# Attention: the transposes of a pair of query tiles, and their products with V, each begun only when the operands of all of them are there

## The chip, the cores and the metric

One core of a Trainium2 chip runs the whole program. The metric is device time in microseconds of one execution, compared as medians. Before the change the median of 3 runs is 2395.19 us (2393.38 to 2398.52).

## The reference, cut to what matters

The program is one step of a two-layer encoder over 2048 prompt frames and 32 sample frames, width 1024. Layer 0 is sliding-window attention, layer 1 a gated DeltaNet. The change touches layer 0 alone. There 16 query heads share 4 key and value heads of width 64. A chunk of 64 frames reads itself and the 128 frames before it:

```python
s = jnp.einsum('bnqkgd,bnskd->bnkgqs', q, k) * (HEAD_DIM ** -0.5)
s = s - slopes * dist                      # ALiBi, then -inf outside the window
m = jnp.maximum(jnp.max(s, axis=-1, keepdims=True), sink)
p = jnp.exp(s - m)
den = jnp.sum(p, axis=-1, keepdims=True) + jnp.exp(sink - m)
o = jnp.einsum('bnkgqs,bnskd->bnqkgd', p / den, v)
y = (o * jax.nn.silu(gate)) @ w_out
```

All is fp32. The big projections (`h @ w_in`, `@ w_out`) are each split into three products of rounded parts.

## The kernel before, in words

**Tiling.** The tokens are cut into 4 slabs of 512 (the second carries the 32 sample frames too). Each slab's attention runs over 20 projection blocks of 128 output columns: for each of two groups of heads a key block, a value block, and four times a query block and a gate block. A block is 24 matmuls of up to 512 columns into bank `pj` (`project`, line 624), so TensorE has a stream of projection work. Output blocks (`out_blocks`, line 865) of an earlier slab are mixed in. Then comes the DeltaNet stage, which does not run the changed function.

**A pair of query tiles.** After each gate block `attention` (line 1188) spawns side jobs: for a prompt slab two calls of `attend` (line 1064), each for two query tiles of 128 frames and the two heads of one index `i`; in the second slab one more, for the 32 sample frames. That makes 64 calls for pairs of tiles and 8 for the sample frames. At most three calls are under way at a time. In one call, in this order:

1. scores into two `ta` banks, bias and row maximum into `s` on VectorE (DVE), one of four units (two tiles times two heads) at a time;
2. exponentials of the four units on ScalarE (ACT), sums into `den`;
3. four `tensor_scalar` on DVE, `s<-s,den`, one for each unit: the scaling by 1/den;
4. for each tile: take a `tb` bank, four transposes of 128x128 (`tb<-con,s`; two key blocks times two heads), one ACT copy of the bank to SBUF (`pt<-tb`), give the bank back, and let the projection go on before the next tile (`yield 0`);
5. for each tile: four products with V (`tc<-pt,vt`, stationary V of 64 columns, so output goes to one half of the partitions), then again `yield 0` before the next tile. Each fp32 product stands as two matmul records, so one tile is 8 records and a pair is 16;
6. `of<-tc,sg` on DVE, rounding on ACT, remainder on GpSimd (POOL), and the call counts as attended.

**What sets the order.** Nothing is issued when the Python code runs. Each call of an engine becomes an `Op` (line 196) in `Order` (line 211), with a rank by the order of emission. A side job is advanced between two projection matmuls (`step`, line 465), by a clock that `Estimate` (line 77) keeps with costs per operation; a bare `yield` there waits until the job's last operation is estimated done, and `yield 0` waits for nothing but lets the projection emit its next matmul first. At the end of a stage `flush` (line 299) plays the engines forward in estimated time: an operation becomes ready when those it depends on have ended plus a lag, and of the ready ones of an engine the lowest rank goes first. That fixes each engine's program order. On the chip each instruction waits for its own semaphores only, in that order.

**Costs in the plan.** `Estimate.COST` (line 88) gives a DVE scaling of 256 columns with a per-partition scalar 68 + 0.52 x 256 + 60 = 261 ns, and an ACT copy of 512 columns from PSUM 52 + 0.83 x 512 = 477 ns; `cost` (line 119) gives a projection matmul of 512 columns 216 ns and knows no price for going from one form of matmul to another.

**Banks.** `BANKS` (line 441) gives `ta` and `tb` two banks each and `tc` one. `bank` (line 516) takes one bank when one is free; `both` (line 523) waits until none is held and takes two. Before the change only the scores use `both`.

Of the kernel before, what the change touches and what calls it, by code (L numbers as in the profile page):

```python
# [3 lines left out]

# [1 line left out]

# [10 lines left out]
P = 128  # L17
# [5 lines left out]
CH = 64  # L23
# [33 lines left out]
class Block:  # L57
# [3 lines left out]
    def __init__(self, src, run, need=None, ahead=None, pre=None, post=None, ks=range(KT)):  # L61
        self.beside = False
        self.src, self.run, self.need, self.ahead, self.pre, self.post, self.ks = src, run, need, ahead, pre, post, ks
# [132 lines left out]
class Op:  # L196


    def __init__(self, engine, call=None, cost=0.0, dma=False):
        self.engine, self.call, self.cost, self.dma = engine, call, cost, dma  # L200
        self.after, self.left, self.ends, self.done, self.rank = [], 0, {}, False, 0


class Place:
# [6 lines left out]
class Order:  # L211
# [9 lines left out]
    def __init__(self, est):  # L221
        self.est = est
        self.ops, self.log, self.places, self.rings = [], {}, {}, {}
        self.free, self.dma, self.rank = dict.fromkeys(self.ENGINES, 0.0), 0.0, 0
        self.lead, self.past = 0, []

    def place(self, pool, tag, bufs, name):
        ring = self.rings.setdefault((id(pool), tag), [])
# [21 lines left out]
    def add(self, op, ins, outs):  # L250
        self.rank += 1
        op.rank = (self.rank - self.lead, self.rank)
        self.ops.append(op)
        waits = {}
        for x, w in [(x, False) for x in ins] + [(x, True) for x in outs]:
            name = x.tensor.name
            if name in self.places:
                self.places[name].ops.append(op)
            elif not name.startswith(SCRATCH):
                continue  # L260
            a = self.region(x)
            bank = x.space == bass.MemoryType.PSUM
            log = []
            for b, bw, o in self.log.get(name, []):
                meet = a[0] < b[1] and b[0] < a[1] and (bank or a[2] < b[3] and b[2] < a[3])
                if o is not op and ((w or bw) and meet or bank and o.engine != op.engine):
                    waits[id(o)] = o
                    if w and a[0] <= b[0] and b[1] <= a[1] and a[2] <= b[2] and b[3] <= a[3]:
                        continue
                log.append((b, bw, o))  # L270
            self.log[name] = log + [(a, w, op)]
        for o in waits.values():
            self.link(o, op)
        if op.engine == "tensor":
            self.past.append((self.est.at("tensor"), op))
        elif op.dma:
            i = bisect.bisect(self.past, min(self.est.at("tensor") - self.EARLY, self.START), key=lambda x: x[0])
            if i:
                self.link(self.past[i - 1][1], op)
# [19 lines left out]
    def flush(self):  # L299

        overs = []
        for p in self.places.values():
            if p.old and p.over is None:
                p.over = Op(None)
                overs.append(p.over)
                for o in p.old.ops:
                    self.link(o, p.over)
                for o in {id(o): o for o in p.ops}.values():
                    self.link(p.over, o)
        self.wait = {e: [] for e in self.ENGINES}  # L310
        ready = {e: [] for e in self.ENGINES}
        for o in [o for o in overs + self.ops if o.left == 0]:
            self.settle(o)
        while any(self.wait.values()) or any(ready.values()):
            when = {e: max(self.free[e], 0.0 if ready[e] else self.wait[e][0][0]) for e in self.ENGINES if ready[e] or self.wait[e]}
            e = min(when, key=when.get)
            now = when[e]
            while self.wait[e] and self.wait[e][0][0] <= now:
                _, rank, o = heapq.heappop(self.wait[e])
                heapq.heappush(ready[e], (rank, o))  # L320
            _, op = heapq.heappop(ready[e])
            op.call()
            if op.dma:
                self.free[e] = now + 60
                self.dma = max(now + 1500, self.dma) + op.cost * (self.CLOSE if now < self.START else 1)
                op.ends = {"dma": self.dma + 500}
            else:
                self.free[e] = now + op.cost
                op.ends = {e: self.free[e]}
            op.start = now  # L330
            self.finish(op)
        assert all(o.done for o in self.ops)
        self.ops = []
# [49 lines left out]
class Kern:  # L383
# [680 lines left out]
    def attend(self, me, i, q, sg, gp, vt, og, m, pairs, keyn, tiles, ocol):  # L1064
# [10 lines left out]
        s = self.t(ap, [P, 4, WIN], "s", bufs=3)[:m]  # L1075
# [3 lines left out]
        banks = yield from self.both("ta")  # L1079
        for a, (qc, kc, lo) in enumerate(pairs):  # L1080
            for n, (part, k) in enumerate(((0, kh), (0, kl), (1, kh))):
                for x, ps in enumerate(banks):
                    rows = slice(x * CH, (x + 1) * CH)
# [26 lines left out]
            nc.vector.tensor_scalar(out=s[:, u, lo:keyn], in0=s[:, u, lo:keyn], scalar1=unit(den, u), scalar2=None, op0=ALU.mult)  # L1110
        yield
        pts = []
        for a, tl in enumerate(tiles):
            ps = yield from self.bank("tb")
            pt = self.t(ap, [P, 2, 2, P], "pt", bufs=4)
            for jj, (blk, vidx, rows) in enumerate(tl):
                for x in range(2):
                    at = (jj * 2 + x) * P
                    self.tp(ps[:rows, at : at + m], s[:, 2 * a + x, blk * P : blk * P + rows])
            if len(tl) == 2 and m == P:  # L1120
                ev = [(pt.rearrange("p a b t -> p (a b t)"), ps)]
            else:
                ev = [(pt[:r, j, :, :m], ps[:r, j * 2 * P : (j + 1) * 2 * P].rearrange("p (x t) -> p x t", x=2)[:, :, :m])
                      for j, (_, _, r) in enumerate(tl)]
            for dst, src in ev:
                nc.scalar.copy(dst, src)
            pts.append((a, pt, tl))
            self.give("tb")
            yield 0
        yield  # L1130
        yield from og.wait()
        po = yield from self.bank("tc")
        for a, pt, tl in pts:
            for x in range(2):
                for jj, (blk, vidx, rows) in enumerate(tl):
                    self.mm(
                        po[x * CH : (x + 1) * CH, a * P : a * P + m], vt[:rows, vidx, x * CH : (x + 1) * CH],
                        pt[:rows, jj, x, :m], jj == 0, jj == len(tl) - 1)
            yield 0
        yield  # L1140
        n = (np_ - 1) * P + m
        of = self.t(ap, [P, 2 * P], "of", bufs=2)
# [806 lines left out]
    def last_outs(self, si, slab, og, over):  # L1949
# [7 lines left out]
        def sink(f, two, y, cols):  # L1957

            ys[f] = two, y
            acc = accs[halves.index(cols)]  # L1960
            add = (lambda st, x, i, first=False, last=False:
                   self.mm(st[:, 0:1], x[:, i * P : (i + 1) * P], self.ones[:, 0:1], first, last))
            if f == 0:
                acc.n, acc.sts, acc.scaled = 0, [], () if acc is accs[0] else (1, 4, 6)
                if acc is accs[0]:
                    for x in ("acc", "rb", "xa"):
                        yield from self.take(x)
                acc.t = self.t(self.xp, [P, 544], "acc" if acc is accs[0] else "rb", bufs=1)[:, : n // 2]
                if acc is accs[1]:
                    for bank in ("ms", "tc"):  # L1970
                        acc.sts.append((yield from self.bank(bank)))
            yield y
            sq = self.t(self.xp, [P, 544], "xa", bufs=3)[:, : n // 2] if f else acc.t
            self.nc.scalar.activation(sq, y[:, cols], AF.Square)
            yield
            if f and not (acc.sts and f >= POOLED):
                (nc.gpsimd if acc.sts else nc.vector).tensor_tensor(out=acc.t, in0=acc.t, in1=sq, op=ALU.add)
            elif f:
                for i, st in enumerate(acc.sts):
                    if f == KT - 1:  # L1980
                        add(st, acc.t, i)
                    add(st, sq, i, f == POOLED, f == KT - 1)
            if f in acc.scaled:
                self.nc.scalar.activation(y[:, cols], y[:, cols], AF.Copy, scale=self.par[:, PC_FG + f : PC_FG + f + 1])
            acc.last = acc.sts[1] if acc.sts else acc.t
            acc.n += 1
# [248 lines left out]
```

## Time and profile before

| | |
|---|---|
| median of 3 runs | 2395.19 us |
| the profiled execution, its own time | 2401.5 us |
| its span, first to last instruction | 2399.7 us |
| mean granted TensorE clock | 0.971 of 2.4 GHz |
| attention stage | about the first 940 us |
| products with V, records (attention only) | 1056, from 50.4 to 932.2 us |
| instructions of the span | 44456 |

The span is 1.8 us shorter than the execution's own time. PE is TensorE's matmuls, PEld its weight loads. In a timeline of PE a row is a run of like matmuls; the start of the next row less the start of this one is what the run took of TensorE's time, since the printed duration holds the pipeline's tail as well. A mark in square brackets at the end of a row is idle time ahead of it and the engine that ended it.

### The profile page before, as it was taken

What the parts mean: (1) busy time and instruction counts of PE and PEld (TensorE: products, weight loads), DVE (VectorE), ACT (ScalarE), POOL (GpSimd) and SP (SyncE); (2) the same over time, 40 slices, a digit from 0 to 9 for tenths busy, and PEclk for the clock granted to TensorE, in tenths of its full rate; (3) what the DMA queues carried; (4) which work ended last, traced back from release to release, by engine and by line L of the source; (5) the groups of instructions that cost most, each with busy time, mean ns of one, the idle gap of its engine ahead of it and who ended that gap; (6) DMA issues with size and microseconds to landing.
All of it is one profiled execution on the core that took longest, in us unless ns stands there. A gap on an engine that the chain in (4) does not pass through costs nothing.

```text
span 2399.7 us, 44456 instructions
## 1 busy us (share of the span) xinstructions
PE 2279.1 (95%) x14759; PEld 1851.9 (77%) x14759; DVE 1644.0 (69%) x5024; ACT 1265.6 (53%) x3792; POOL 864.4 (36%) x1044
## 2 busy tenths in 40 slices
PE   8999999899999999999999999999999999999997
PEld 5667888797778777777779798876798777777776
DVE  6765465726562546488888768888786888886876
ACT  5555465636553555355666454674554466445533
POOL 4566555565554333223322122331312222222222
PEclk9998999999999999999999999998999989999998
DMA  7565755476525124644334564334456634466541
GB/s 253 167 190 181 240 181 177 150 252 213 176 89 164 63 64 135 199 159 139 121 109 133 181 226 154 120 99 136 138 162 213 213 113 139 138 212 214 159 141 67
DMA packets 222832, 382.75 MB, mean 159 GB/s; under 512 B 29922, under 2 KB 45194, under 8 KB 222602
## 3 DMA queue, kind: packets, MB, share of 16 engines
q1 hardware_dynamic: 220154, 377.75, 49.4%
q8 instruction: 116, 1.90, 0.3%
q10 hardware_dynamic: 2448, 2.16, 0.3%
q14 instruction: 114, 0.93, 0.1%
HBM read 311.63 MB, written 68.19 MB: 158 GB/s over the span
## 4 chain that ended last, share of the span: by engine, by line
PE 57%; DVE 24%; ACT 7%; issue 3%; DMA 3%; POOL 2%; SPq 0%; DVEq 0%; ACTq 0%; POOLq 0%
PE pj L185 41%; PE tb L185 6%; PE ta L185 5%; PE tc L185 4%; DVE cy L185 3%; DVE s L185 3%; DVE sub L185 2%; DVE tl L185 2%; ACT s L185 1%; DVE ml L185 1%; ACT ta L185 1%; DVE r L185 1%; DVE mx L185 1%; DVE md L185 1%; DVE xa L185 1%
## 5 line engine op out<-in xcount | busy, mean ns | idle before, releaser
L185 PE MATMUL pj<-hk,wh 128*128 128x512 f32 (+1 forms) x8184 | 1796.7, 365 | 23.1 <-DVE xr L185 6.8
L185 PEld LDWEIGHTS pj<-hk,wh 128*128 128x128 f32 x8184 | 1331.4, 192 | 237.2 <-issue 22.9
L185 POOL TENSOR_TENSOR wh<-wr,wh 128x512 fp32r<-128x512 f32 x224 | 295.3, 1321 | 333.2 <-ACT wh L185 282.0
L185 DVE SCALAR_TENSOR_TENSOR cy<-cx,cw,cy 128x512 f32<-128x512 f32 x360 | 230.8, 651 | 45.0 <-ACT cy L185 40.3
L185 ACT CAST wh<-wr 128x512 fp32r<-128x512 f32 x224 | 137.7, 617 | 215.3 <-PE pj L185 164.3
L185 ACT ACTIVATE s<-s,mx 128x256 f32<-128x256 f32 (+1 forms) x272 | 132.0, 487 | 32.3 <-DVE mx L185 32.0
L185 ACT ACTIVATE qs<-tb,egq 64x128 f32<-64x128 f32 x264 | 95.8, 363 | 88.4 <-DVE r L185 76.0
L185 DVE TENSOR_SCALAR s<-s,den 128x256 f32<-128x256 f32 (+1 forms) x272 | 133.6, 542 | 1.3
L185 DVE TENSOR_TENSOR sub<-ml,tl 128x60 f32<-128x60 f32 (+24 forms) x527 | 126.5, 240 | 10.2
L185 ACT ACTIVATE cx<-cy 128x512 f32<-128x512 f32 (+1 forms) x96 | 61.1, 636 | 130.9 <-DVE cy L185 104.4
L185 DVE TENSOR_TENSOR tl<-tl,sub 128x60 f32<-128x60 f32 (+24 forms) x527 | 122.8, 233 | 10.0
L185 POOL TENSOR_TENSOR pr<-pr,ph 128x512 fp32r<-128x512 f32 x82 | 111.2, 1356 | 40.6 <-ACT ph L185 37.7
L185 DVE CUSTOM_DVE_ANT_0 s<-ta,bias 128x256 f32<-128x256 f32 (+1 forms) x272 | 96.3, 405 | 39.3 <-PE ta L185 38.0
L185 POOL COPY cx<-hist 128x3 f32<-128x3 f32 x96 | 26.7, 278 | 264.3 <-DVE kq L185 62.7
L185 DVE TENSOR_TENSOR xr<-pj,xr 128x512 f32<-128x512 f32 (+1 forms) x72 | 41.2, 577 | 108.3 <-PE pj L185 72.1
L185 POOL TENSOR_TENSOR so<-so,mhalf 128x4 f32<-128x4 f32 x33 | 36.8, 1114 | 218.0 <-DVE so L185 190.2
L185 DVE SCALAR_TENSOR_TENSOR r<-tb,nbk,vb 64x128 f32<-64x128 f32 x264 | 91.8, 348 | 29.9 <-PE tb L185 25.3
L185 ACT ACTIVATE qs<-o 128x128 f32<-128x128 f32 x132 | 40.7, 308 | 133.4 <-DVE o L185 128.1
L185 ACT COPY cx<-pj 128x512 f32<-128x512 f32 (+2 forms) x149 | 64.1, 446 | 78.9 <-PE pj L185 63.5
L185 PE MATMUL tc<-pt,vt 128*64 128x128 f32 (+2 forms) x1056 | 91.3, 289 | 12.1 <-ACT pt L185 11.3
L185 PE MATMUL tb<-st,kq 128*128 128x128 f32 x512 | 95.7, 289 | 6.4 <-DVE st L185 5.7
L185 PEld LDWEIGHTS tb<-st,kq 128*128 128x128 f32 x512 | 83.4, 196 | 21.3 <-DVE st L185 13.1
(242 smaller groups left out, 3578.6 us busy)
## 6 DMA issues: line engine op xcount, KB each, us to landing
wh<-xswwd SPq DMA_DIRECT2D x528, 256.0 KB, 2.9
wr<-in_wa SPq DMA_DIRECT2D x160, 256.0 KB, 2.9
wh<-xswwdo SPq DMA_DIRECT2D x112, 256.0 KB, 2.9
pr<-in_wd SPq DMA_DIRECT2D x66, 256.0 KB, 4.0
xswwd<-ph SPq DMA_DIRECT2D x66, 256.0 KB, 2.7
xswwd<-pr SPq DMA_DIRECT2D x66, 256.0 KB, 3.6
wr<-in_wao SPq DMA_DIRECT2D x64, 256.0 KB, 2.9
xa<-in_x SPq DMA_DIRECT2D x48, 256.0 KB, 3.3
```

Of the source, the lines that this page charges most:

```text
L185: self.order.add(Op(self.name, lambda: call(*args, **kw), cost, op == "dma_start"), ins, outs)
```

## The change

`Order` gets groups. `together()` opens one: a group is an `Op` without an engine, and every TensorE operation that is added while it is open depends on it, while it depends on all that these wait for outside the group. So in the plan no operation of the group is ready before all of their operands are, and their banks free. The group is only in the plan: no instruction and no semaphore is added on the chip. In `attend`, the two `tb` banks are taken at once with `both`, the eight transposes of a pair form one group, then the two copies follow and both banks are given back; the products with V of the pair form a second group. The two `yield 0` go.

```diff
+    @contextmanager
+    def together(self):
+
+        self.gang = Op(None)
+        self.ops.append(self.gang)
+        yield
+        self.gang = None
...
+        if self.gang and op.engine == "tensor":
+            op.gang = self.gang
+            self.link(op.gang, op)
         for o in waits.values():
             self.link(o, op)
+            if op.gang and o.gang is not op.gang:
+                self.link(o, op.gang)
...
                 for o in {id(o): o for o in p.ops}.values():
                     self.link(p.over, o)
+                    if o.gang:
+                        self.link(p.over, o.gang)
...
         pts = []
-        for a, tl in enumerate(tiles):
-            ps = yield from self.bank("tb")
+        banks = yield from self.both("tb")
+        with self.issue.together():
+            for a, (ps, tl) in enumerate(zip(banks, tiles)):
+                for jj, (blk, vidx, rows) in enumerate(tl):
+                    for x in range(2):
+                        at = (jj * 2 + x) * P
+                        self.tp(ps[:rows, at : at + m], s[:, 2 * a + x, blk * P : blk * P + rows])
+        for a, (ps, tl) in enumerate(zip(banks, tiles)):
             pt = self.t(ap, [P, 2, 2, P], "pt", bufs=4)
-            for jj, (blk, vidx, rows) in enumerate(tl):
-                for x in range(2):
-                    at = (jj * 2 + x) * P
-                    self.tp(ps[:rows, at : at + m], s[:, 2 * a + x, blk * P : blk * P + rows])
...
             pts.append((a, pt, tl))
+        for _ in banks:
             self.give("tb")
-            yield 0
         yield
         yield from og.wait()
         po = yield from self.bank("tc")
-        for a, pt, tl in pts:
-            for x in range(2):
-                for jj, (blk, vidx, rows) in enumerate(tl):
-                    self.mm(
-                        po[x * CH : (x + 1) * CH, a * P : a * P + m], vt[:rows, vidx, x * CH : (x + 1) * CH],
-                        pt[:rows, jj, x, :m], jj == 0, jj == len(tl) - 1)
-            yield 0
+        with self.issue.together():
+            for a, pt, tl in pts:
+                for x in range(2):
+                    for jj, (blk, vidx, rows) in enumerate(tl):
+                        self.mm(
+                            po[x * CH : (x + 1) * CH, a * P : a * P + m], vt[:rows, vidx, x * CH : (x + 1) * CH],
+                            pt[:rows, jj, x, :m], jj == 0, jj == len(tl) - 1)
         yield
```

## Rows read from the trace of the kernel before

**Rows 1.** The page: busy time by engine, and the chain that ended last.
```profile
PE 2279.1 (95%) x14759; PEld 1851.9 (77%) x14759; DVE 1644.0 (69%) x5024; ACT 1265.6 (53%) x3792; POOL 864.4 (36%) x1044
...
PE 57%; DVE 24%; ACT 7%; issue 3%; DMA 3%; POOL 2%; SPq 0%; DVEq 0%; ACTq 0%; POOLq 0%
```

**Rows 2.** Busy by stretch: window, length, PE, PEld, DVE, ACT, POOL, PEclk, DMA, GB/s.
```profile
0.00:940.00 940.00, 891.13 (x5729) 711.91 (x5730) 517.87 (x1514) 509.16 (x1337) 487.66 (x420) 0.98 0.52 167
940.00:2400.00 1460.00, 1387.94 (x9032) 1140.02 (x9030) 1126.16 (x3511) 756.44 (x2455) 376.70 (x624) 0.97 0.49 154
460.00:475.00 15.00, 11.10 (x56) 7.64 (x54) 12.36 (x37) 8.60 (x29) 8.65 (x9) 0.77 0.46 141
711.00:717.00 6.00, 6.00 (x53) 4.64 (x52) 2.13 (x6) 3.15 (x8) 2.01 (x2) 1.00 0.23 72
780.00:935.00 155.00, 154.24 (x992) 116.74 (x991) 86.41 (x314) 87.05 (x247) 56.15 (x50) 1.00 0.21 67
```

**Rows 3.** PE timeline, products with V: the first and the last run of 116.
```profile
50.45 0.44 PE L185 MATMUL tc<-pt,vt 128*64 128x128 f32 x4 [1.30 <-ACT pt L185]
...
931.92 0.67 PE L185 MATMUL tc<-pt,vt 128*64 128x128 f32 x8
```

**Rows 4.** PE timeline of 782 to 796 us: two pairs of tiles, in part.
```profile
782.76 5.12 PE L185 MATMUL pj<-hk,wh 128*128 128x512 f32 x21
787.72 0.60 PE L185 MATMUL tb<-con,s 128*128 128x128 f32 x4
788.08 0.48 PE L185 MATMUL pj<-hk,wh 128*128 128x512 f32 x1
788.39 0.60 PE L185 MATMUL tb<-con,s 128*128 128x128 f32 x4
788.75 1.17 PE L185 MATMUL pj<-hk,wh 128*128 128x512 f32 x4
789.85 1.14 PE L185 MATMUL tc<-pt,vt 128*64 128x128 f32 x16
790.92 0.51 PE L185 MATMUL pj<-hk,wh 128*128 128x512 f32 x1
...
792.94 0.67 PE L185 MATMUL tc<-pt,vt 128*64 128x128 f32 x8
793.53 0.50 PE L185 MATMUL pj<-hk,wh 128*128 128x512 f32 x1
793.97 0.67 PE L185 MATMUL tc<-pt,vt 128*64 128x128 f32 x8
794.56 1.66 PE L185 MATMUL pj<-hk,wh 128*128 128x512 f32 x6
```

**Rows 5.** PE timeline of 316 to 319 us: eight transposes in one run.
```profile
317.77 1.04 PE L185 MATMUL tb<-con,s 128*128 128x128 f32 x8
318.56 0.62 PE L185 MATMUL pj<-hk,wh 128*128 128x272 f32 x3
```

**Rows 6.** Waits of PE, 0 to 940 us: for whom, us in total, times, longest.
```profile
PE tb L185 <- DVE s L185: 13.5, 19, 2.1
PE tc L185 <- ACT pt L185: 11.3, 17, 1.5
```

**Rows 7.** Tile s on DVE: duration in ns, minimum, median, maximum; first and last start.
```profile
L185 DVE TENSOR_SCALAR s<-s,den x272: 273/348/1468, 45.5 to 928.2; 128x256 f32<-128x256 f32 x120, 128x128 f32<-128x128 f32 x8, 32x160 f32<-32x160 f32 x8
```

**Rows 8.** Tile pt on ACT, the same columns.
```profile
L185 ACT COPY pt<-tb x144: 196/580/607, 50.0 to 930.7; 128x512 f32<-128x512 f32 x120, 128x256 f32<-128x256 f32 x8, 128x64 f32<-128x64 f32 x8, 32x64 f32<-32x64 f32 x8
```

**Rows 9.** PE timeline of 711.5 to 717 us.
```profile
712.20 1.14 PE L185 MATMUL tc<-pt,vt 128*64 128x128 f32 x16
713.27 1.09 PE L185 MATMUL tb<-con,s 128*128 128x128 f32 x8
...
714.98 1.15 PE L185 MATMUL tc<-pt,vt 128*64 128x128 f32 x16
```

**Rows 10.** PE timeline of 465 to 473 us.
```profile
468.07 0.48 PE L185 MATMUL tb<-con,s 128*128 128x128 f32 x1 [2.07 <-DVE s L185]
```

More of the change, by code (lines that the diff above doesn't have):

```diff
@@ L2 @@
 import heapq
-from contextlib import ExitStack
+from contextlib import ExitStack, contextmanager
 import numpy as np
@@ L224, in __init__ @@
         self.free, self.dma, self.rank = dict.fromkeys(self.ENGINES, 0.0), 0.0, 0
-        self.lead, self.past = 0, []
+        self.lead, self.past, self.gang = 0, [], None
+    @contextmanager
[3 more added lines that the diff above has]
+        yield
+        self.gang = None
     def place(self, pool, tag, bufs, name):
```

## The prediction

> **What bounds the kernel now.** I read the page first, then the stretches, then TensorE's waits in the attention stage, and last the order of single runs of matmuls on PE. The page shows PE busy for 95% of the span, and the chain that ended last lies on PE for 57% [rows 1]; the reader should see that no other engine is near. Cut in two, the stage with attention (0 to 940 us) has PE busy 891.13 of 940 us [rows 2], so what shortens PE's own stream there shortens the stage, unless something else takes its place. In its last slab PE is busy for 154.24 of 155 us [rows 2]: there the stage is nothing but PE's stream. In the waits of that stage two belong to the changed code: transposes that waited for the scaling `s<-s,den` (13.5 us in 19 waits) and products with V that waited for the copy `pt` (11.3 us in 17) [rows 6]. The timeline then shows what the waits don't: what a change of form costs on PE.
>
> **The change part by part.** *Products with V.* Counted along the PE timeline from the first to the last run [rows 3], the 1056 records of products stand in 116 uninterrupted runs: 21 of 16 records (both tiles together), 82 of 8, the rest of 2 to 14. There are 64 pairs and 8 sample calls, so one run for each would be 72: 44 runs fewer. The price of a run more: two runs of 8 with one projection matmul between take from 792.94 to 794.56, that is 1.62 us. One run of 16 takes from 789.85 to 790.92, 1.07 us. A projection matmul in an undisturbed stretch takes (787.72 - 782.76) / 21 = 0.236 us [all rows 4]. Ahead of either form stands the same entry, and behind it the same exit, so joined work costs 1.07 + 0.236 = 1.306 us and a join saves 1.62 - 1.31 = 0.31 us. It is a loss of TensorE time in going in and out of the half-width form, with nothing beside it on PE that could hide it. 44 x 0.31 = 13.8 us. Some of the runs are parted by transposes or by several projection matmuls; I price them alike, since entry and exit are paid there too.
>
> *Transposes.* Four, a projection matmul, four: from 787.72 to 788.75, 1.03 us, less 0.236 for the matmul is 0.79 us [rows 4]. Eight in one run: from 317.77 to 318.56, 0.79 us [rows 5]. Going in and out of this form costs nothing beyond what the first projection matmul behind pays once more or once less, so joining them is worth 0, though the code makes as much of it as of the products.
>
> *The waits.* The group waits only in the plan. While it is not ready, projection matmuls of a later rank go first, so on PE nothing is queued behind a waiting instruction that was not before; the order changes, and with it where PE can be caught early. The plan counts 261 ns for a scaling that took 348 in the median and up to 1468 [rows 7], and 477 ns for a copy that took 580 [rows 8]; such an order runs ahead of the chip, and that is what the waits are. In a group the first product of a tile comes no earlier than the plan's end of the second copy, 477 ns later than its own, so the wait for the first copy loses up to that much, and the second copy ends beside the first tile's products (0.59 us, half of the pair [rows 4]). For the transposes the last one waits as before, and the first seven stand in front of it. Bounds: below, both waits go, -24.8 us [rows 6]. Above, each of 64 pairs stands still for the whole second copy of 0.58 us [rows 8], +37 us. The nearest rows are the joined runs that exist: the one at 789.85 and that at 712.20 start without idle time [rows 4, 9], and in the stretch where most pairs' first half is so joined, PE's idle time is 0.76 us in 155 [rows 2]. I take -4 us, about a third of the 11.3 us of the products, because those joined runs are the ones in which nothing was late, and count nothing for the transposes.
>
> *Banks and copies.* A call now needs both `tb` banks at once, and its copies come back to back on ACT. The first copy still follows the first four transposes, so both copies are done about 0.44 + 0.58 + 0.58 = 1.6 us after the first transpose starts, plus a semaphore's way each. In the run at 787.72 the products began 2.13 us after the first transpose [rows 4], so this chain gets no longer. If it did, the next call's scores are its cover: ACT is busy 509 and DVE 518 of 940 us [rows 2], and three calls are under way. DMAs are neither added nor moved past another; those tied in the plan to a matmul move with it by less than a pair's length, 2 us. What is late next, where a wait goes, is the scaling and rounding behind the products, with two calls more to hide it.
>
> *Clock.* In 460 to 475 us PE had 0.77 of its clock, so 0.23 x 15 = 3.5 us were lost, in a stretch where a transpose had stood 2.07 us for the scaling [rows 2, 10]. In the whole stage the clock is 0.98, some 19 us lost. Fewer waits should give back some of it, but I count 0, as I can't say which.
>
> *A rule that speaks against it.* In 711 to 717 us PE went through 16 records of products, 8 transposes in one run and 16 records again, all at a granted clock of 1.00, the upper of its two levels [rows 2, 9]. The Trainium skill says, in "TensorE: Matmul & The Clock Gate", section "Part 4: PE-mode transpose", that a transpose does not count as busy to the clock gate, so longer runs of them should bring half clock. By that rule the change would lose time; the trace of that stretch does not bear it out. What it would do here as a mechanism is priced below.
>
> *The DeltaNet stage* (940 to 2400 us) has the same code. Its plan starts from other engine times, so its order may shift; its clock of 0.97 stands for 0.03 x 1460 = 44 us lost [rows 2], and a fifth of that, 9 us either way, is what I allow for it.
>
> **Sum.** -13.8 - 4 = -17.8 us. Against the profiled execution's own 2401.5 us (span 2399.7 and 1.8 around it) that is 2383.7 us. The profiled execution lies 6.3 us above the median of the runs, so against the median: 2395.2 - 17.8 = 2377.4 us.
>
> **The rivals.** (a) *The waits go with it.* All 24.8 us of rows 6 vanish instead of 4, at the same joins: 2395.2 - 13.8 - 24.8 = 2356.6 us. For it: the plan's errors in rows 7 and 8 are of the size of the delay that the group adds. Against: most waits are longer than 0.48 us in the mean (11.3 / 17 = 0.66), so they can only shrink.
>
> (b) *The second copy stands in the open; slower.* Place: the first product of each pair, which in the plan now waits for two copies of 477 ns and on the chip for two of 580, with other ACT work between. Price 0.58 us a pair [rows 8]. It decides from 13.8 / 0.58 = 24 of 64 pairs on; with all 64 the time is 2395.2 - 13.8 + 37.1 = 2418.5 us. For it: the chain from transposes to products is the one with waits today. Against: the joined runs of today start without idle time [rows 4, 9].
>
> (c) *The clock falls in the longer runs.* If a pair's run of transposes and products brought PE to its lower level as the stretch of 460 to 475 us did, at 3.5 us each [rows 2], four pairs would cancel the gain and 16 would make 2395.2 - 13.8 + 56 = 2437 us. This is what the page named above would have. Rows 9 at a clock of 1.00 speak against it.
>
> (d) *It does not do what it says.* Projection matmuls of a lower rank that become ready in between still part the runs, or a run now borders on another form so that entry and exit are paid all the same: 2393 to 2397 us. For it: ranks still decide, and the group only sets when its parts are ready. Against: the parts of a group carry ranks in a row.
>
> **How the numbers follow.** A measurement of this kernel can tell 0.2%, 4.8 us, from no change. The forecast (joins at full price, waits between 0 and -8, DeltaNet 9 either way; its own range 2364 to 2390) has 0.64, (a) 0.08, (b) 0.10, (c) 0.05, (d) 0.13. Faster: 0.62 of the forecast, 0.08 of (a), 0.02 of (d), 0.72 in all. Slower: 0.07 of (b), 0.04 of (c), 0.02 of (d), 0.13. Within 0.2%: the rest, 0.15. The range of 8 in 10 goes from 2362, which leaves out most of (a), to 2399, which holds (d) and the milder half of (b).
>
> **What would show it.** Right: the products' records in about 72 runs, nearly all of 16 for a pair, each taking some 1.07 us; transposes in runs of 8 at 0.79 us; the projection's undisturbed pace unchanged; the last product of the attention stage some 14 to 18 us earlier than 932 us; the DeltaNet stage of the same length. Wrong: more than 90 runs of products (d); PE's waits of products for `pt` above 20 us (b); a granted clock in 0 to 940 us under 0.97 beside these runs (c). A gain that is in the attention stage and is lost again after 940 us would break the sum at its last step.

## The result, and the profile after

The changed kernel takes 2375.28 us in the median of 4 runs (2372.83 to 2376.40), the kernel before 2396.86 us beside it: ratio 0.9909, 95% interval 0.9888 to 0.9930. It is 21.6 us faster; 17.8 were forecast. The profiled execution took 2376.4 us (before 2401.5), its span 2374.6 us. Run again on another chip, with the experiments, it took 2374.16 us, ratio 0.9903 (0.9883 to 0.9924).

First the page of the changed kernel, busy time by engine and the chain that ended last, as in [rows 1].

```profile
PE 2252.8 (95%) x14759; PEld 1843.9 (78%) x14759; DVE 1639.6 (69%) x5024; ACT 1262.2 (53%) x3792; POOL 862.9 (36%) x1044
...
PE 56%; DVE 28%; ACT 7%; issue 4%; DMA 3%; POOL 2%; SPq 0%; DVEq 0%; ACTq 0%; POOLq 0%
```

The counts of instructions of each engine are the same; only the order differs. PE is busy 26.3 us less. The PE timeline of the changed kernel has the first and last products with V here, against [rows 3].

```profile
50.80 1.14 PE L185 MATMUL tc<-pt,vt 128*64 128x128 f32 x12
...
907.88 1.15 PE L185 MATMUL tc<-pt,vt 128*64 128x128 f32 x16
908.95 1.20 PE L185 MATMUL pj<-hk,wh 128*128 128x512 f32 x4
```

Between them the products stand in 73 runs (before 116), 56 of them of 16 records, and the transposes in 73 (before 129). The last product ends at 908.95 us; before it was 931.92 + 0.59 = 932.51 [rows 3, 4]. So the attention stage is 23.6 us shorter, and what follows takes 1465.6 us against 1467.2: the DeltaNet stage has the same instructions in the same order and gave back nothing. The stretches of the changed kernel, cut at that point (columns as in [rows 2]):

```profile
0.00:909.00 909.00, 862.78 (x5708) 702.77 (x5708) 506.92 (x1505) 502.50 (x1330) 483.99 (x417) 0.99 0.53 172
909.00:2374.00 1465.00, 1390.03 (x9053) 1141.12 (x9052) 1132.68 (x3520) 759.72 (x2462) 378.92 (x627) 0.97 0.48 155
```

Two pairs on PE's timeline of the changed kernel, against [rows 4]:

```profile
801.61 1.03 PE L185 MATMUL tb<-con,s 128*128 128x128 f32 x8
802.40 1.85 PE L185 MATMUL pj<-hk,wh 128*128 128x512 f32 x7
804.18 1.14 PE L185 MATMUL tc<-pt,vt 128*64 128x128 f32 x16
805.26 0.50 PE L185 MATMUL pj<-hk,wh 128*128 128x512 f32 x1
805.60 1.04 PE L185 MATMUL tb<-con,s 128*128 128x128 f32 x8
806.39 1.64 PE L185 MATMUL pj<-hk,wh 128*128 128x512 f32 x6
807.96 1.14 PE L185 MATMUL tc<-pt,vt 128*64 128x128 f32 x16
809.03 1.43 PE L185 MATMUL pj<-hk,wh 128*128 128x512 f32 x5
```

Each pair is one run of 8 transposes (802.40 - 801.61 = 0.79 us) and one of 16 records (809.03 - 807.96 = 1.07 us), with no idle mark. PE's waits in the attention stage of the changed kernel, against [rows 6]:

```profile
PE tb L185 <- DVE s L185: 16.0, 20, 2.5
...
PE tc L185 <- ACT pt L185: 6.9, 5, 4.7
...
PE tb L185 <- ACT pt L185: 2.7, 3, 1.3
```

The kernel before has one such wait beside the two of [rows 6]:

```profile
PE tb L185 <- ACT pt L185: 1.0, 1, 1.0
```

Here the reader is to see what did not happen: the waits for `s` and `pt` sum to 25.6 us, and they summed to 25.8 before. Products wait less, transposes more. One wait of 4.7 us is most of the products' share.

### The profile page after: what moved, and what is told of

The parts are those of the page before. It is cut to its first block, busy times and chain, and to the rows that moved or that the text cites. A ratio compares the mean times of both kernels' runs of the same rounds, so it can differ in the third digit from the quotient of the medians.

```text
span 2374.6 us, 44457 instructions
## 1 busy us (share of the span) xinstructions
PE 2252.8 (95%) x14759; PEld 1843.9 (78%) x14759; DVE 1639.6 (69%) x5024; ACT 1262.2 (53%) x3792; POOL 862.9 (36%) x1044
## 4 chain that ended last, share of the span: by engine, by line
PE 56%; DVE 28%; ACT 7%; issue 4%; DMA 3%; POOL 2%; SPq 0%; DVEq 0%; ACTq 0%; POOLq 0%
PE pj L185 39%; PE tb L185 6%; PE ta L185 5%; PE tc L185 4%; DVE cy L185 4%; DVE s L185 3%; DVE sub L185 3%; DVE tl L185 3%; ACT s L185 2%; DVE ml L185 2%; ACT ta L185 1%; DVE xa L185 1%; DVE r L185 1%; DVE md L185 1%; DVE mx L185 1%
## 5 line engine op out<-in xcount | busy, mean ns | idle before, releaser
L185 PE MATMUL pj<-hk,wh 128*128 128x512 f32 (+1 forms) x8184 | 1770.1, 364 | 26.9 <-DVE xr L185 8.6
L185 DVE TENSOR_TENSOR tl<-tl,sub 128x60 f32<-128x60 f32 (+24 forms) x527 | 122.3, 232 | 10.1
L185 DVE SCALAR_TENSOR_TENSOR r<-tb,nbk,vb 64x128 f32<-64x128 f32 x264 | 91.7, 348 | 29.6 <-PE tb L185 25.1
L185 PE MATMUL tb<-con,s 128*128 128x128 f32 (+2 forms) x528 | 77.7, 280 | 18.9 <-DVE s L185 16.0
```

The source lines that it names most:

```text
L185: self.order.add(Op(self.name, lambda: call(*args, **kw), cost, op == "dma_start"), ins, outs)
```

## The experiments

All were timed beside the kernel before on the same chip (its median 2396.7 to 2398.5 us), but `full_width` stands on one run. Waits are PE's in the attention stage, for `s` and `pt`, in the one profiled execution of each kernel.

**Products alone.** The transposes, banks and copies as before the change, the products in their group.

```diff
-        banks = yield from self.both("tb")
-        with self.issue.together():
...
+        for a, tl in enumerate(tiles):
+            ps = yield from self.bank("tb")
...
+            self.give("tb")
+            yield 0
```

> Only the products with V are grouped; the transposes are taken tile by tile as before the change. Products in 72 runs, transposes in 140. Theory A (the time is that of going in and out of the products' form, 0.31 us a run; transposes cost nothing): as the changed kernel, 2375 us, within 4. Rival C (the joined transposes carry a share of the gain): half or more of 21 us is lost, 2386 us or more.

2392.1 us, ratio 0.9978 (0.9962 to 0.9995), though the products stand in 72 runs. Theory A failed here: most of the gain is missing. The waits of this kernel say where it went:

```profile
PE tb L185 <- DVE s L185: 23.3, 31, 2.7
...
PE tb L185 <- ACT pt L185: 2.9, 3, 1.6
...
PE tc L185 <- ACT pt L185: 1.8, 2, 1.0
```

Transposes wait for the scaling 23.3 us, 9.8 more than before the change. Products wait 9.5 us less for `pt`, so these three rows alone do not hold the loss; all of PE's idle time in the stage grew by 9.5 us, from 47.9 to 57.4, with smaller waits of other kinds in it.

**Transposes alone.** The products tile by tile as before.

```diff
-        with self.issue.together():
-            for a, pt, tl in pts:
...
+        for a, pt, tl in pts:
...
+            yield 0
```

> Only the transposes are grouped; products with V tile by tile as before the change. Products in 116 runs, transposes in 76. Theory A: 43 runs more than the changed kernel at 0.31 us, 13 us, so 2389 us, and up to 2397 if the clock's share goes with it. Rival C: 2380 us or less.

2373.2 us, ratio 0.9911 (0.9888 to 0.9934): as much gain as the whole change, with products still in 116 runs. Theory A failed again. The waits of this kernel:

```profile
PE tb L185 <- DVE s L185: 11.1, 17, 1.0
...
PE tb L185 <- ACT pt L185: 2.3, 2, 1.3
...
PE tc L185 <- ACT pt L185: 0.4, 2, 0.2
```

Products hardly wait any more (0.4 us, before 11.3). By the medians, with the transposes joined, joining the products was worth nothing that could be measured (2373.2 and 2374.2 us, on different chips), though it takes 43 runs away. The granted clock bears on that: four of the six executions here had 0.983 or more and took 2368.75 to 2373.69 us, the two at 0.979 took 2377.87 and 2381.87. The changed kernel had 0.979 in the median, and its execution at 0.979 took 2374.16 us.

**Without the groups in the plan.** Both banks at once, no `yield 0`, nothing else.

```diff
-        with self.issue.together():
+        if True:
```

> The changed kernel without the groups in the plan: both banks at once and no projection matmul let in between by the emission, but each transpose and product may be placed as soon as its own operands are planned. Products in 83 runs, transposes in 86. Theory A: 10 runs more, 3 us, so 2378 us. Rival B (it is the later start that the group gives, so that less is begun early and waits): the gain is mostly lost, 2390 us or more, and PE's waits of transposes and products rise by more than 10 us.

2381.9 us, ratio 0.9941 (0.9920 to 0.9961). Rival B fell: the emission alone brings some 15 of the 22 us, and the waits are those of the changed kernel (15.7 and 6.9 us). Theory A's 2378 us was 4 us too low.

**Products in four groups**, a matmul let in between.

```diff
-        with self.issue.together():
-            for a, pt, tl in pts:
-                for x in range(2):
+        for a, pt, tl in pts:
+            for x in range(2):
+                with self.issue.together():
...
+                yield 0
```

> The changed kernel with the products of a pair in four groups, a projection matmul let in between by the emission. Products in 204 runs, transposes in 72. Theory A: 131 runs more at 0.31 us, 41 us, so 2416 us. Rival B (a group's later start is the gain, and that remains): 2375 to 2385 us.

2432.2 us, ratio 1.0151 (1.0128 to 1.0174), 58 us above the changed kernel for 131 runs more. Rival B fell clearly. The price is 0.44 us a run, above my 0.31, though PE's idle time in the stage even fell, from 46.2 to 30.4 us; the work itself grew by more. PE's timeline of this kernel shows why:

```profile
810.17 0.67 PE L185 MATMUL tc<-pt,vt 128*64 128x128 f32 x8
810.77 0.50 PE L185 MATMUL pj<-hk,wh 128*128 128x512 f32 x1
811.20 0.65 PE L185 MATMUL tc<-pt,vt 128*64 128x128 f32 x4
811.78 0.51 PE L185 MATMUL pj<-hk,wh 128*128 128x512 f32 x1
```

A run of 4 records takes 0.58 us and one of 8 takes 0.60: four records go to one half of the partitions, eight to both, and the halves overlap. So this cut also parts what ran side by side.

**Transposes let apart one by one**, products grouped.

```diff
-        with self.issue.together():
...
                     self.tp(ps[:rows, at : at + m], s[:, 2 * a + x, blk * P : blk * P + rows])
+                    yield 0
```

> The changed kernel, its products grouped, but the eight transposes of a pair let apart one by one, a projection matmul between them: 368 runs of transposes where the changed kernel has 73. Theory A (going in and out of the transposes' form costs nothing): 2375 us, or up to 2392 where the early ones wait, as with the products alone grouped. Rival C (each run costs 0.31 us as one of products does): 295 runs more, 2466 us.

2372.5 us, ratio 0.9900 (0.9885 to 0.9914). Rival C fell: 295 runs more of transposes cost nothing that could be measured. PE's timeline of this kernel has eight transposes with seven projection matmuls between them:

```profile
800.56 0.27 PE L185 MATMUL tb<-con,s 128*128 128x128 f32 x1
...
802.99 0.27 PE L185 MATMUL tb<-con,s 128*128 128x128 f32 x1
803.02 2.78 PE L185 MATMUL pj<-hk,wh 128*128 128x512 f32 x11
```

That is 2.46 us, less 7 x 0.236 is 0.81 us, where eight in one run take 0.79. The time also says that in the changed kernel it is not the joined run of transposes that helps. Apart, but each a matmul later than the one before and all of them ahead of the copies, they do as well; waits are 10.1 us for `s` and 4.9 for `pt`.

**Full width.** The kernel before, in its own order; the plan keeps its old cost for these products.

```diff
-                        po[x * CH : (x + 1) * CH, a * P : a * P + m], vt[:rows, vidx, x * CH : (x + 1) * CH],
+                        po[:, a * P : a * P + m], vt[:rows, vidx, :],
```

> The kernel before, its order unchanged, but each product with V takes the stationary V of both heads, 128 columns, so that the second head of a pair overwrites the first (the attention output is then that of one head alone). Theory A: the price of a run belongs to the half-width form; 0.11 us more for each of 528 products, 58 us, but in the timeline two runs of 8 with a projection matmul between take no longer than one of 16 and a matmul, and some 30 us of entries and exits go: 2425 us, within 10. Rival D (it belongs to any fp32 product between rounded ones): the 0.31 us stand in the timeline, 2455 us.

One run: 2419.65 us (theory A 2425 within 10, rival D 2455). PE's timeline of this kernel, one run of 16 and then two of 8:

```profile
798.85 1.95 PE L187 MATMUL tc<-pt,vt 128*128 128x128 f32 x16
800.55 0.49 PE L187 MATMUL pj<-hk,wh 128*128 128x512 f32 x1
```

```profile
802.46 1.05 PE L187 MATMUL tc<-pt,vt 128*128 128x128 f32 x8
803.27 0.48 PE L187 MATMUL pj<-hk,wh 128*128 128x512 f32 x1
803.59 1.05 PE L187 MATMUL tc<-pt,vt 128*128 128x128 f32 x8
804.40 0.94 PE L187 MATMUL pj<-hk,wh 128*128 128x512 f32 x3
```

Two of 8 with a matmul between take 804.40 - 802.46 = 1.94 us; one of 16 takes 1.70, and 0.236 for the matmul makes the same 1.94. The 0.31 us is gone: it is the price of the half-width form, not of fp32 among rounded matmuls. The wider product itself takes (1.70 - 1.07) / 8 = 0.08 us more, where 0.11 was expected, which is why the time lies below 2425.

**The plan told the truth about two costs.** Theory A2, formed after the first four runs: the work that a join saves is real, but a PE that is quicker than the chip's DVE and ACT against the plan meets their late results, and the time comes back as waits. The plan counted 261 ns for a scaling and 477 for a copy ([rows 7, 8] have 348 and 580 as medians).

```diff
         fixed, each, more = self.COST[engine]
+        name = out.tensor.name
+        if name.startswith("s_") and op == "tensor_scalar":
+            return 350.0
+        if name.startswith("pt_") and n == 512:
+            return 580.0
```

> The changed kernel, with the plan told 350 ns for a scaling of s (it counted 261) and 580 ns for a copy of 512 columns to pt (it counted 477). Theory A2: joining the products saves some 17 to 20 us of PE's own work, and part of it is eaten by waits, since a PE that is nearer to its plan catches DVE and ACT behind theirs; with the costs corrected PE's waits for s and pt fall from 25.6 us to 15 or less and the time to 2362 to 2370 us. Rival B2: the waits come from the scalings that take over 1.3 us, which no mean cost foresees; waits stay over 20 us, the time 2371 to 2379 us.

2364.3 us, ratio 0.9858 (0.9837 to 0.9880), the fastest of all kernels here. The waits of this kernel:

```profile
PE tb L190 <- DVE s L190: 7.5, 14, 1.0
...
PE tc L190 <- ACT pt L190: 1.2, 2, 0.8
...
PE tb L190 <- ACT pt L190: 0.5, 1, 0.5
```

9.2 us instead of 25.6: theory A2 held, rival B2 fell.

The same edit in the kernel before the change:

> The kernel before the change, with the same two costs corrected in the plan. Theory A2: the waits for s and pt fall from 24.8 us to about 12, the products' runs stay over 100, and the time is 2383 to 2390 us: the waits' share of the gain without the joins. Rival B2: 2393 to 2400 us.

2391.5 us, ratio 0.9978 (0.9965 to 0.9990), between the two. Waits fell only to 18.7 us (12.2 and 6.5), and the products' runs rose to 127. True costs alone take a quarter of the change's gain.

The next three ran beside the changed kernel once more.

> The changed kernel again, on the same chip as the next three. By its first four runs 2372 to 2378 us.

2374.16 us.

**Transposes alone, true costs** (the edits of the second and the seventh experiment together).

> The kernel with the transposes alone grouped, and the two costs of the plan corrected (350 and 580 ns). Products in 127 runs, where the changed kernel with these costs has 77. Theory A3 (joined products save PE's work at 0.31 to 0.4 us a run in any case, and that was hidden before by waits that took its place): 50 runs more, 2380 to 2384 us. Rival E (with the transposes joined, joining the products is worth nothing): 2360 to 2368 us.

2378.9 us, ratio 0.9930 (0.9908 to 0.9953). Against 2364.3 us with the products joined too, 50 runs cost 14.6 us, 0.29 us a run, with waits for `s` and `pt` alike (9.1 and 9.2 us). Some of it may be no price of runs: the profiled execution has 5.0 us more in two waits of products for `of`. Theory A3 held but for the 1 us below its bound; rival E fell. The joins are worth their price once waits no longer swallow it. The two stood on different chips, with the kernel before at 2398.5 and 2397.1 us.

**Products alone, true costs.**

> The kernel with the products alone grouped, and the two costs of the plan corrected. Products in 72 runs, transposes in 131. Theory A3 (the transposes' group is worth only the waits that it avoids, and a true plan avoids them as well): 2364 to 2372 us. Rival F (only the group of the transposes takes their waits away): 2380 us or more, with PE's waits for s above 18 us.

2384.2 us, ratio 0.9945 (0.9925 to 0.9965), waits for `s` 15.1 us. Neither held: true costs win back 8 us here, not the 20 or more of theory A3, and the waits stay under rival F's 18. Why the tile-by-tile transposes keep waiting even so is open.

**The mean instead of the median:** `return 540.0` for a scaling.

> The changed kernel, with the plan told 540 ns for a scaling, the mean with the slow ones in it, and 580 ns for a copy. Theory A3: waits for s and pt fall from 9.2 us to 6 or less, the time to 2356 to 2363 us. Rival: the group comes later than it need, nothing is won over the median's cost, 2361 to 2368 us.

2368.1 us, ratio 0.9879 (0.9854 to 0.9903): no better than the median's cost, as the rival had it. Waits fell a little, to 8.9 us, not to 6.

## Why the prediction was right, and which step was not

**The total and the place were right.** 21.6 us against 17.8. Of the 25.1 us between the two profiled executions 23.6 lie in the attention stage, and nothing was lost later. The last product came 23.6 us earlier, not the 14 to 18 forecast.

The traces allow the stage to be cut in three. PE's idle time is the time in which it is not busy. The granted clock stands in a trace as stretches at one of its two levels, 1.2 and 2.4 GHz. In the changed kernel one projection matmul followed another after 0.427 us at the lower level and 0.234 at the upper (medians), so I take 0.45 of PE's busy time at the lower level as lost, an estimate. What is left is PE's work at the upper level. In us, one execution of each kernel:

| kernel | runs of products | stage | PE idle | lost to the clock | PE's work |
|---|---|---|---|---|---|
| before | 116 | 932.5 | 47.9 | 18.0 | 866.6 |
| changed | 73 | 909.0 | 46.2 | 9.5 | 853.2 |
| products alone | 72 | 924.5 | 57.4 | 12.7 | 854.4 |
| transposes alone | 116 | 913.8 | 40.6 | 8.5 | 864.6 |
| changed, true costs | 77 | 896.8 | 32.7 | 8.6 | 855.5 |
| transposes alone, true costs | 127 | 916.6 | 37.9 | 9.5 | 869.1 |

**The joins: the price was right, and so was what carries it.** 73 runs instead of the 72 forecast; 43 x 0.314 = 13.5 us of PE's stream. The last column agrees: 13.4 us less for 43 runs, 12.2 for 44 with the products alone, 13.6 for 50 with true costs, and 2.0 where the runs stayed 116. Two experiments bear it out by independent ways: `full_width` takes the price away with the half-width form, and with true costs 50 runs are worth up to 0.29 us each.

**The step that failed is the sum itself**, "-13.8 - 4", as a sum of terms that stand by themselves, together with "count nothing for the transposes". The transposes have no price as a form (`t_eight`), but their place decides how long PE stands idle. With the products alone joined, 12.2 us of work were saved and idle time grew by 9.5; the kernel gained some 5 us. With the transposes alone joined, the work hardly changed, but idle time fell by 7.3 us and the clock's share by 9.5, and the kernel gained 21 to 24 us. With both, transposes wait 16.0 us for `s` instead of 11.1, products 6.9 for `pt` instead of 0.4, and idle time is 5.6 us longer than with the transposes alone. That a quicker PE meets late results is the reading which the true costs support: with them both kernels wait alike, and the joins show in the time. But 4.7 us are one wait at one place, and no run removes that wait alone.

**The waits.** The -4 us was right for the products (11.3 to 6.9) and wrong for the sum, which hardly fell (25.8 to 25.6); all of PE's idle time fell by 1.7 us.

**The clock, counted 0.** Its share fell by 8.5 us: 13.4 of work, 1.7 of idle time and 8.5 of clock are the 23.6 us that the stage lost. That is an account that closes for two executions, not an experiment: no run here changed the clock by itself. Part of it is the execution that happened to be profiled. The kernel before had a clock of 0.971 there and 0.976 in the median beside the experiments, and within one kernel a higher clock goes with a shorter time (2388.02 us at 0.982, 2402.74 at 0.973). The changed kernel had 0.979. So a total near the forecast, with waits that fell less than forecast and a clock counted 0, is in part luck.

**The rivals.** (d) is excluded by the 73 runs, (a) by the waits. (c) did not come; the granted clock rose. (b) came at one place, not as one copy in the open but as another call's work ahead of it. The timeline of the changed kernel, PE, DVE and ACT, there:

```profile
178.78 0.82 PE L185 MATMUL tb<-con,s 128*128 128x128 f32 x6
...
180.56 1.29 DVE L185 TENSOR_SCALAR mx<-mx 128x4 f32<-128x4 f32 x1
...
181.88 0.51 ACT L185 ACTIVATE s<-s,mx 128x256 f32<-128x256 f32 x1 [1.87 <-DVE mx L185]
...
183.38 0.49 ACT L185 ACTIVATE s<-s,mx 128x256 f32<-128x256 f32 x1
...
183.87 0.82 ACT L185 COPY pt<-tb 128x256 f32<-128x256 f32 x2
...
184.27 1.60 PE L185 MATMUL tc<-pt,vt 128*64 128x128 f32 x12 [4.68 <-ACT pt L185]
```

The transposes are done by 179.6 us, but ACT has the exponentials of the next call ahead of the two copies in its program order, and those wait for a tiny DVE operation that took 1.29 us. The products stand 4.68 us, with the projection queued behind them, and the stretch around it runs at a clock of 0.74 (the second row is the kernel before):

```profile
175.00:215.00 40.00, 31.11 (x193) 25.46 (x192) 31.36 (x71) 22.89 (x62) 25.76 (x21) 0.74 0.51 161
175.00:215.00 40.00, 37.48 (x205) 29.10 (x206) 30.55 (x83) 21.89 (x66) 22.36 (x18) 0.79 0.48 145
```

That the wait brings the clock down is not shown: the kernel before has 0.79 in the same stretch without it, and the changed kernel, run again, 0.83 with it.

**What stays open.** The split of the 21.6 us between the two halves has no one answer: each half gains alone (some 5 and 21 to 24 us), and the two together no more than the second. `t_only` and the changed kernel come out so near because less idle time and a higher clock stand against more work, but their executions scatter by 4 to 13 us, and at a like clock `t_only` is some us slower. Whether the joined transposes themselves raise the clock is not shown.

## What to carry to other kernels

A run of matmuls in another array form can have a price for going in and out that no duration shows: take it from the start of one run to the start of the next, and compare a parted with a joined run. When the order comes from a plan, a saving on the bound engine can come back as waits for the other engines where the plan counts those too cheap, so sum the waits of all neighbours, not only those of the rows that change. Test each half of a change alone and both together: here the halves did not add up, and the half that I had priced at nothing alone brought as much as both. Before two kernels are called equal, compare the granted clock of their executions too.

## What the runs showed of the hardware

- Going in and out of the 64-column form costs 0.31 us a run at a projection matmul's side; eight transposes at full width cost 0.79 us in one run and 0.81 in eight (295 runs more cost nothing that could be measured).
- Products of two heads that write the two halves of the partitions overlap: 8 records to both halves took 0.60 us, 4 records to one half 0.58.
- A scaling of 256 columns beside a GpSimd `tensor_tensor` can take four times as long. In the changed kernel 45 of 240 took over 1 us, each beside one; 47 others touched one too and took at most 0.55 us. The timeline of the changed kernel, POOL and DVE:

```profile
185.87 1.27 POOL L185 TENSOR_TENSOR wh<-wr,wh 128x512 fp32r<-128x512 f32 x1 [2.81 <-DMA xa<-in_x]
185.87 1.42 DVE L185 TENSOR_SCALAR s<-s,den 128x256 f32<-128x256 f32 x1
```

  It took 1.42 us against the 0.348 us of the median [rows 7], and ended about with the GpSimd operation. The Trainium skill, "SBUF — State Buffer", section "SBUF: two separate sides", has the two engines share a pair of ports that some DVE operations and those of GpSimd lock for a whole instruction; this row agrees.
